# First x rows of a one-core decoder trunk: the norm columns in a transfer of their own, the first weight block in halves, two identity products ahead on TensorE

## The chip, the core and the metric

The kernel runs on one core of a Trainium2 chip. The metric is device time in microseconds (us) of one execution. Before the change three runs gave 1355.26 to 1356.71 us, with a median of 1356.11 us.

## What is computed

The reference is one layer of a hybrid decoder on 1024 tokens of width 1024, in f32. Cut to what the first stage of the kernel works on:

```python
def rmsnorm(x, w):
    y = x * lax.rsqrt(jnp.mean(x * x, axis=-1, keepdims=True) + EPS)
    return y * w

xn = rmsnorm(x, norm_mix_w[l])
proj = xn @ w_in[l]                 # 1024 x 4352
da_q, da_k, da_v, sw_q, sw_k, sw_v, g_da, g_sw = split_cols(proj)
...
merged = sigmoid(g_da) * (y_da @ w_br_da) + sigmoid(g_sw) * (y_sw @ w_br_sw)
x = x + merged @ w_mix_out
x = x + conv_ffn(rmsnorm(x, norm_ffn_w), w_up, conv_w, conv_b, w_down)
return rmsnorm(x, norm_final_w)
```

Behind the projection come differential attention with four heads, a sliding-window attention, the merge, and a gated MLP with a causal convolution. Only the start of the projection is changed.

## The kernel before, in words

**Layout.** The host lays x out transposed, in eight rows of tiles `xT[kc]` of 128 channels x 1024 tokens (512 KB each), and each weight matrix in blocks of 128 output columns (`w_in[m]`, 128 x 8 x 128, 512 KB). All small vectors lie in one array `vecs` of 128 partitions x 469 columns (234.5 KB). Its columns 0 to 7 are `norm_mix_w`, one column for each row of tiles; the other columns hold the other norms, the convolution, the sinks and the lambda vectors.

**Products in f32.** An f32 operand is split in two float32r parts, high and low. ScalarE writes the high part (a cast or a multiply), VectorE the low part (operand minus high part). A product is then three TensorE matmuls: high x high, low x high and high x low. In `load()` (L294) ScalarE writes `xh = x * w` (L301) and VectorE writes `xl` (L302), both with the column `wcol(kc)` of `vecs` (L317). In `load_w()` (L122) a weight block is transferred (L119) and split: `wh` on ScalarE (L129), `wl` on VectorE (L131). `split()` (L754) does the same for two given tiles. `blocks()` (L271) issues six matmuls for a weight block and an x row, three for each half of 512 tokens (L276 to L278).

**Order of the first stage, `project()` (L250).** The x rows are taken in the order 0, 4, 1, 5, 2, 6, 3, 7. The first is transferred in two halves of 512 tokens, with the whole first weight block between the two; the others are transferred whole. After row 4 the second weight block is loaded and multiplied with rows 0 and 4, after row 5 the third. Three weight blocks times eight rows times six are 144 matmuls, which accumulate in six PSUM banks. Beside them `square()` (L306) makes the sum of squares and multiplies x by the norm weights in place (L310 to L315), and `diffs()` and `parts()` (L280, L289) prepare differences and sums of x rows for the later pairs of weight blocks, which are multiplied with seven products instead of eight (`prods`). The sums over the partitions are taken by `col_sums` (L158: eight matmuls with f32 operands), then `rstd` is made and spread over the partitions (L173).

**PSUM.** The pool `psA` holds eight banks, taken in turn by one tag: six for the accumulations, then `ssq`, then the gate halves and the products of the pairs. When it closes, the attention's pools `psS`, `psG` and `psT` take the banks over, each new tile waiting for the last reader of the tile that was there.

**Queues and order.** x rows and weights are issued on SyncE's queue (SP), `vecs` on ScalarE's (L196). Waits and the order of instructions on each engine are put in by a framework that works from the dependences, with the place in the program as the priority: an instruction may be put ahead of others that stand before it in the program and whose inputs come later. `nsink` and `subw` (L442, L444), written at the beginning of the attention, read `vecs` on VectorE and stand first on that engine. `load_w` uses raw buffers of which there are three, and `xr` has six buffers, so later transfers wait for buffers.

The program's start (L184 to L196): the identity, `ones` and `mhalf` are made on GpSimd, `warm` makes ScalarE load its table, and `vecs` is transferred.

Of the kernel before, what the change touches and what calls it, by code (L numbers as in the profile page):

```python
# [10 lines left out]
F32 = mybir.dt.float32  # L11
F32R = mybir.dt.float32r
# [5 lines left out]
P = 128  # L18
D = 1024
T = 1024  # L20
KC = D // P
# [5 lines left out]
RAW = 3  # L27
# [15 lines left out]
class Trunk:  # L43
# [132 lines left out]
    def run(self):  # L176
        nc, tc = self.nc, self.tc
        with ExitStack() as ctx:

            for side, n in (("left", LPAD), ("right", RPAD)):  # L180
                pad = ctx.enter_context(tc.tile_pool(name=f"pad_{side}", bufs=1, side=side))
                pad.tile([P, n // 4], F32, name=f"pad_{side}_t")
            self.cp = ctx.enter_context(tc.tile_pool(name="cp", bufs=1))
            self.st = ctx.enter_context(tc.tile_pool(name="st", bufs=4))  # L184
            self.dp = ctx.enter_context(tc.tile_pool(name="dp", bufs=1, space=DRAM))
            self.ident = self.cp.tile([P, P], F32, name="ident")
            make_identity(nc, self.ident)
            self.ones = self.cp.tile([P, 1], F32, name="ones")
            nc.gpsimd.memset(self.ones, 1.0)
            self.mhalf = self.cp.tile([P, 8], F32, name="mhalf")  # L190
            nc.gpsimd.memset(self.mhalf, -0.5)
            self.vecs = self.cp.tile([P, NVEC], F32, name="vecs")

            warm = self.cp.tile([P, 1], F32, name="warm")
            nc.scalar.activation(warm, self.ones, AF.Exp)
            nc.scalar.dma_start(self.vecs, self.vecs_d)  # L196
            self.rstd = self.cp.tile([P, T], F32, name="rstd")
            self.gd = self.dp.tile([16, P, T], F32, name="gd")
            self.x2d = self.dp.tile([8, P, T], F32, name="x2d")
            self.hd = self.dp.tile([NF, P, T], F32, name="hd")  # L200
            self.yd = self.dp.tile([8, P, T], F32, name="yd")
            self.wp = ctx.enter_context(tc.tile_pool(name="wp", bufs=2))
            self.qd = self.dp.tile([18, 2, P, T], F32, name="qd")
            self.xctx = ExitStack()
            self.xp = self.xctx.enter_context(tc.tile_pool(name="xp", bufs=1, side="right", reuse_waits="tile"))
            self.plan()
            self.project()
            self.pctx = ExitStack()
            self.psS = self.pctx.enter_context(tc.tile_pool(name="psS", bufs=2, space=PSUM, reuse_waits="tile"))
            self.psG = self.pctx.enter_context(tc.tile_pool(name="psG", bufs=2, space=PSUM, reuse_waits="tile"))  # L210
            self.psT = self.pctx.enter_context(tc.tile_pool(name="psT", bufs=2, space=PSUM, reuse_waits="tile"))
            gctx = ExitStack()
            self.gpool = gctx.enter_context(tc.tile_pool(name="gp", bufs=2, reuse_waits="tile"))
            self.attention()
            self.rest(gctx)
# [34 lines left out]
    def project(self):  # L250
# [6 lines left out]
        with ExitStack() as ctx:  # L257
# [8 lines left out]
            rows = [k + 4 * i for k in range(4) for i in range(2)]  # L266
            xr, ws = {}, []
            bank = lambda: self.tl(psA, [P, H2], "t")
            ps = [[bank() for _ in range(2)] for _ in range(3)]

            def blocks(n, kcs):  # L271
# [21 lines left out]
            with tc.tile_pool(name="xrp", bufs=6, reuse_waits="tile") as xrp:  # L293
                def load(kc, cuts=((0, T),)):  # L294

                    x = xr[kc] = self.tl(xrp, [P, T], "xr")
                    for a, b in cuts:
                        nc.sync.dma_start(x[:, a:b], self.xT[kc, :, a:b])
                        if not ws:
                            ws.append(self.load_w(*self.wsrc.pop(0)))  # L300
                        nc.scalar.mul(self.xh[kc][:, a:b], x[:, a:b], wcol(kc))  # L301
                        nc.vector.scalar_tensor_tensor(self.xl[kc][:, a:b], x[:, a:b], wcol(kc), self.xh[kc][:, a:b].bitcast(F32), ALU.mult, ALU.subtract)  # L302
                    for n in range(len(ws)):
                        blocks(n, [kc])

                def square(kc):  # L306

                    x = xr[kc]
                    if kc == rows[0]:
                        nc.scalar.activation(acc, x, AF.Square)  # L310
                    else:
                        sq = self.tl(self.sfp[0], [P, T], "sf")
                        nc.scalar.activation(sq, x, AF.Square)
                        nc.vector.tensor_tensor(acc, acc, sq, ALU.add)
                    nc.scalar.mul(x, x, wcol(kc))  # L315

                wcol = lambda kc: self.vecs[:, C_NM + kc:C_NM + kc + 1]  # L317
                for i, kc in enumerate(rows[:6]):
                    load(kc, ((0, H2), (H2, T)) if i == 0 else ((0, T),))
                    if i in (1, 3):  # L320
                        ws.append(self.load_w(*self.wsrc.pop(0), pool=(self.uw, "sh", "sl") if i == 3 else None))
                        blocks(len(ws) - 1, rows[:i + 1])
                for kc in rows[:2]:
                    square(kc)
                diffs(0)
                for kc in rows[6:]:
                    load(kc)
                for kc in rows[2:]:
                    square(kc)
                ssq = bank()  # L330
                self.col_sums(ssq, [acc], NB, 0)
                rs = self.rstd_cols(ssq, 8, D)
                wg = self.next_w()
                pg = [bank()]
                for hf in range(2):
                    self.mm3(pg[0], wg, self.xact, 0, *((range(5), True, False), (range(5, KC), False, True))[hf])
                    self.spread(ssq, rs, hf * 4)
                    nc.vector.tensor_copy(self.rstd[:, hf * H2:(hf + 1) * H2], ssq)
                parts(0)
                for k in range(1, 4):  # L340
                    if k == 3:

                        us = [self.tl(xrp, [P, T], "xr") for _ in range(3)]
                        for hf in range(2):
                            for u, hv in zip(us, ps):
                                cols = slice(hf * H2, (hf + 1) * H2)
                                nc.vector.tensor_tensor(u[:, cols], hv[hf], self.rstd[:, cols], ALU.mult)
                    diffs(k)
                    parts(k)
                pg.append(bank())  # L350
                self.mm3(pg[1], wg, self.xact, 1)
                for m, u in zip(self.plain, us):
                    self.keep(m, u, (xrp, "xr"))
# [857 lines left out]
```

## Time and profile before

| | us |
|---|---|
| median of 3 runs (lowest, highest) | 1356.11 (1355.26, 1356.71) |
| the profiled execution, its own time | 1356.2 |
| its span, first to last instruction | 1354.3 |
| TensorE busy | 1335.0 (99%) |
| VectorE busy | 1009.8 (75%) |
| ScalarE busy | 603.9 (45%) |
| GpSimd busy | 483.1 (36%) |

The profile is of one execution. Times in it are microseconds from its first instruction; 1.9 us of the execution's own time lie outside the span. In a row of the timeline stand the start, the duration, the engine, the line of the kernel, the operation, output and inputs, and in brackets how long the engine had been idle and what released it. PE is TensorE, PEld its weight loads, DVE VectorE, ACT ScalarE, POOL GpSimd; ACTq and SPq are rows of transfers being issued. A view of stretches gives the busy time of each engine between two times, the granted TensorE clock, the share of time that the 16 DMA engines were busy, and GB/s. The chain of waits is followed back from the last instruction to what released each step.

### The profile page before, as it was taken

The page shows a single profiled execution, that of the slowest core. Times are in us where ns is not written, and L with a number is a line of the kernel's source. Part 1 is how long each engine was busy: PE and PEld are TensorE (multiplying, and loading weights), DVE is VectorE, ACT ScalarE, POOL GpSimd, SP SyncE. Part 2 cuts the span into 40 slices and gives each one's busy share as a digit, 9 for nine tenths or more (in the row PEclk, how much of TensorE's full clock was granted, in tenths as well). Part 3 has the DMA queues.
Part 4 walks back from the last instruction along what each step waited for, and adds up shares of the span by engine and source line. Part 5 has one row for each costly group of instructions (what it writes and reads, how often), then busy time and mean ns, then how long its engine had stood idle before and what let it go on. Part 6 is the DMA issues. An engine that isn't in the chain of part 4 may idle for free.

```text
span 1354.3 us, 17160 instructions
## 1 busy us (share of the span) xinstructions
PE 1335.0 (99%) x6304; PEld 1103.6 (81%) x6304; DVE 1009.8 (75%) x1454; ACT 603.9 (45%) x942; POOL 483.1 (36%) x350
## 2 busy tenths in 40 slices
PE   7999999999999999999999999999999999999997
PEld 6888888888887777878888888888888888888886
DVE  8846775388898875355689888888888898986454
ACT  8422232376667664334444334433443345433343
POOL 0436651010102125741455565555555611231011
PEclk9999999999999999999999999999999999999999
DMA  6334443966554235334422222122212248651342
GB/s 255 140 113 164 143 156 114 272 174 175 156 133 144 77 116 219 117 119 136 166 82 88 71 91 94 62 79 93 93 63 83 92 141 311 215 177 64 94 134 85
DMA packets 62470, 179.50 MB, mean 133 GB/s; under 512 B 6833, under 2 KB 15153, under 8 KB 62385
## 3 DMA queue, kind: packets, MB, share of 16 engines
q1 hardware_dynamic: 50928, 160.98, 36.7%
q10 hardware_dynamic: 11456, 17.41, 3.5%
q8 instruction: 50, 0.82, 0.2%
q14 instruction: 36, 0.29, 0.1%
HBM read 129.61 MB, written 48.76 MB: 132 GB/s over the span
## 4 chain that ended last, share of the span: by engine, by line
PE 62%; DVE 17%; POOL 7%; issue 7%; DMA 4%; ACT 3%; POOLq 0%; DVEq 0%; SPq 0%; ACTq 0%
PE t L836 7%; PE t L837 7%; PE t L835 7%; POOL us L965 3%; PE y L996 3%; PE d L996 3%; PE sc L568 3%; PE g L150 2%; PE g L151 2%; DVE c L958 2%; PE g L152 2%; DVE wl L112 2%; DMA gr<-gd 2%; PE sc L151 2%; PE sc L152 2%
## 5 line engine op out<-in xcount | busy, mean ns | idle before, releaser
L970 ACT ACTIVATE c<-us,vecs 128x1024 f32<-128x1024 f32 x44 | 54.8, 1248 | 163.2 <-POOL us L965 160.0
L965 POOL TENSOR_TENSOR us<-us,rstd 128x1024 f32<-128x1024 f32 x42 | 100.7, 2414 | 52.8 <-DVE wl L131 34.3
L110 ACT CAST sh<-sf 128x1024 fp32r<-128x1024 f32 x62 | 64.9, 1051 | 106.2 <-POOL sf L97 61.8
L129 ACT CAST wh<-raw 128x1024 fp32r<-128x1024 f32 (+2 forms) x60 | 60.7, 1012 | 104.8 <-PE sc L151 33.1
L971 DVE SCALAR_TENSOR_TENSOR c<-us,vecs,c 128x1024 f32<-128x1024 f32 x44 | 67.1, 1527 | 51.9 <-ACT c L970 51.9
L131 DVE TENSOR_TENSOR wl<-raw,wh 128x1024 fp32r<-128x1024 f32 (+2 forms) x60 | 75.3, 1256 | 39.1 <-ACT wh L129 29.3
L96 POOL TENSOR_TENSOR sf<-rv 128x512 f32<-128x512 f32 x30 | 42.5, 1417 | 166.7 <-DMA rv<-in_w_up 73.2
L112 DVE TENSOR_TENSOR sl<-sf,sh 128x1024 fp32r<-128x1024 f32 x62 | 88.3, 1426 | 8.2 <-ACT sh L110 8.2
L167 POOL TENSOR_TENSOR rs<-ms,mhalf 128x8 f32<-128x8 f32 (+2 forms) x9 | 14.5, 1614 | 159.1 <-DVE ms L165 148.5
L150 PE MATMUL g<-xh,wh 128*128 128x512 f32 x176 | 70.7, 402 | 0.1
L152 PE MATMUL g<-xh,wl 128*128 128x512 f32 x176 | 70.4, 400 | 0.0
L151 PE MATMUL g<-xl,wh 128*128 128x512 f32 x176 | 70.4, 400 | 0.0
L98 POOL TENSOR_TENSOR sf<-raw,rv 128x512 f32<-128x512 f32 x30 | 41.6, 1386 | 59.9 <-DVE sl L112 59.9
L572 DVE CUSTOM_DVE_ANT_0 L<-sc,bias 128x128 f32<-128x128 f32 (+7 forms) x64 | 47.7, 752 | 17.4 <-PE sc L568 14.1
L551 POOL MEMSET aT<- 128x128 f32 x32 | 6.1, 204 | 152.0 <-PE t L597 101.6
L573 ACT ACTIVATE L<-L,sm 128x128 f32<-128x128 f32 (+7 forms) x64 | 49.6, 778 | 20.7 <-DVE sm L572 18.2
L97 POOL TENSOR_TENSOR sf<-sf,raw 128x512 f32<-128x512 f32 x31 | 58.0, 1870 | 1.6
L972 DVE SCALAR_TENSOR_TENSOR c<-us,vecs,c 128x1024 f32<-128x1024 f32 x44 | 56.2, 1279 | 0.6
L725 POOL TENSOR_TENSOR gr<-gr,rstd 128x1024 f32<-128x1024 f32 x16 | 39.4, 2467 | 41.4 <-DMA gr<-gd 41.2
L112 DVE TENSOR_TENSOR wl<-raw,wh 128x1024 fp32r<-128x1024 f32 (+1 forms) x35 | 52.8, 1508 | 0.1
L151 PE MATMUL sc<-ml,wh 128*128 128x512 f32 x128 | 50.1, 391 | 0.6 <-DVE ml L746 0.6
L568 PE MATMUL sc<-u,u 128*128 128x512 f32 (+2 forms) x192 | 49.8, 359 | 0.1
(444 smaller groups left out, 4351.4 us busy)
## 6 DMA issues: line engine op xcount, KB each, us to landing
u<-qd SPq DMA_DIRECT2D x72, 256.0 KB, 6.1
raw<-in_w_down SPq DMA_DIRECT2D x27, 512.0 KB, 3.7
raw<-in_w_in SPq DMA_DIRECT2D x25, 512.0 KB, 4.4
hr<-hd SPq DMA_DIRECT2D x50, 256.0 KB, 5.3
raw<-in_w_up SPq DMA_DIRECT2D x23, 512.0 KB, 3.6
hd<-c SPq DMA_DIRECT2D x22, 512.0 KB, 2.8
rv<-in_w_up SPq DMA_DIRECT2D x21, 512.0 KB, 3.5
gr<-gd SPq DMA_DIRECT2D x16, 512.0 KB, 3.6
```

Of the source, the lines that this page charges most:

```text
L112: nc.vector.tensor_tensor(lo, src, hi.bitcast(F32), ALU.subtract)
L131: self.lo = (eng or nc.vector).tensor_tensor(wl, raw, wh.bitcast(F32), ALU.subtract)
L150: nc.tensor.matmul(ps, wh[:, kc + o, :], ah, start=first and n == 0, stop=False)
L151: nc.tensor.matmul(ps, wh[:, kc + o, :], al, start=False, stop=False)
L152: nc.tensor.matmul(ps, wl[:, kc + o, :], ah, start=False, stop=last and n == len(kcs) - 1)
L568: nc.tensor.matmul(sc[:, lo + n0:lo + n1], qs, k[c][part][:, n0:n1], start=part == 0, stop=part == 1)
L835: nc.tensor.matmul(ps, ah[:, k, :], bh, start=first and n == 0, stop=False, skip_group_check=skip)
L836: nc.tensor.matmul(ps, ah[:, k, :], bl, start=False, stop=False, skip_group_check=skip)
L837: nc.tensor.matmul(ps, al[:, k, :], bh, start=False, stop=last and n == len(ks) - 1, skip_group_check=skip)
L965: i = (nc.vector if m % NF == 0 else nc.gpsimd).tensor_tensor(us[:, 2:], us[:, 2:], self.rstd, ALU.mult)
L971: nc.vector.scalar_tensor_tensor(c, us[:, 1:T + 1], cw[1], c, ALU.mult, ALU.add)
L996: nc.tensor.matmul(ps, v[:, n, :], x, start=n == i == 0, stop=n == len(js) - 1 and i == 2)
```

## The change

Three edits, all ahead of the second x row. The transfer of `vecs` is cut in two: columns 0 to 7 alone, issued ahead of `warm`, and the other 461 columns, written in the program behind the split of the first weight block's second half, both on ScalarE's queue. The first weight block is transferred and split in two halves of four row tiles each: x half 0, weight half 0, x half 1, weight half 1, each 256 KB, and each weight half is split behind the x half that came before it. And a new PSUM tile `busy` is taken ahead of the six accumulators, and two matmuls write the product of the identity with itself, repeated four times (128 x 512, f32), into it; nothing reads it.

```diff
             self.vecs = self.cp.tile([P, NVEC], F32, name="vecs")
+            nc.scalar.dma_start(self.vecs[:, :KC], self.vecs_d[:, :KC])
             warm = self.cp.tile([P, 1], F32, name="warm")
             nc.scalar.activation(warm, self.ones, AF.Exp)
-            nc.scalar.dma_start(self.vecs, self.vecs_d)
...
             bank = lambda: self.tl(psA, [P, H2], "t")
+            busy = bank()
+            for _ in range(2):
+                nc.tensor.matmul(busy, self.ident, self.ident.unsqueeze(1).to_broadcast([P, 4, P]), start=True, stop=True)
             ps = [[bank() for _ in range(2)] for _ in range(3)]
...
                     for a, b in cuts:
                         nc.sync.dma_start(x[:, a:b], self.xT[kc, :, a:b])
-                        if not ws:
-                            ws.append(self.load_w(*self.wsrc.pop(0)))
+                        k0 = a // P if len(cuts) > 1 else None
+                        if k0 == 0:
+                            raw, wh, wl = (self.tl(self.wp, [P, KC, P], t, dt, **kw) for t, dt, kw in (("raw", F32, {"bufs": RAW}), ("wh", F32R, {}), ("wl", F32R, {})))
+                            ws.append((wh, wl))
+                            src = self.wsrc.pop(0)[0]
+                        if k0 is not None:
+                            nc.sync.dma_start(raw[:, k0:k0 + 4], src[:, k0:k0 + 4])
                         nc.scalar.mul(self.xh[kc][:, a:b], x[:, a:b], wcol(kc))
                         nc.vector.scalar_tensor_tensor(self.xl[kc][:, a:b], x[:, a:b], wcol(kc), self.xh[kc][:, a:b].bitcast(F32), ALU.mult, ALU.subtract)
+                        if k0 is not None:
+                            self.split(wh[:, k0:k0 + 4], wl[:, k0:k0 + 4], raw[:, k0:k0 + 4])
+                        if k0 == 4:
+                            nc.scalar.dma_start(self.vecs[:, KC:], self.vecs_d[:, KC:])
```

## The prediction

> **What bounds the kernel now.** I read the page first, then the table of stretches for the start, then the chain of waits, then TensorE's own rows.
>
> ```profile
> span 1354.3 us, 17160 instructions
> PE 1335.0 (99%) x6304; PEld 1103.6 (81%) x6304; DVE 1009.8 (75%) x1454; ACT 603.9 (45%) x942; POOL 483.1 (36%) x350
> ...
> 0.00:4.00 4.00, 0.00 (x0) 0.00 (x0) 0.00 (x0) 1.49 (x2) 0.77 (x8) 1.00 0.54 153
> 4.00:6.70 2.70, 0.00 (x0) 0.00 (x0) 0.98 (x3) 1.76 (x3) 0.00 (x0) 1.00 0.96 366
> 6.70:10.70 4.00, 3.85 (x9) 2.27 (x9) 3.24 (x4) 4.00 (x6) 0.00 (x0) 1.00 1.02 409
> 10.70:27.00 16.30, 16.30 (x72) 13.52 (x73) 16.20 (x17) 16.30 (x17) 0.00 (x0) 1.00 0.79 300
> ```
>
> TensorE is busy 99% of the span, and from 10.7 on without a gap. So what the start gains or loses is carried to the end, as long as nothing behind it eats it. The change touches only the first 10.7 us, where three other things are full: the DMA engines (0.96 and 1.02 of the time), and from 6.7 ScalarE, which stays full to 27.0. The chain of waits says which of them decides:
>
> ```profile
> 1.19 4.45 DMA raw<-in_w_in
> 5.66 1.04 ACT wh L129
> 6.71 0.62 ACT xh L301
> 7.33 0.95 ACT rstd L310
> 8.28 1.05 ACT xh L301
> 9.35 1.29 DVE xl L302
> 10.69 0.50 PE t L277
> ```
>
> It does not run over TensorE before 10.69. It runs over the weight block's landing at 5.64, ScalarE's queue up to the high part of row 4 (8.28), and VectorE's low part of row 4 (9.35). What TensorE does meanwhile stands in its rows and its waits:
>
> ```profile
> 6.76 0.80 PE L276 MATMUL t<-xh,wh 128*128 128x512 f32 x1 [6.76 <-ACT wh L129]
> ...
> 9.04 0.63 PE L277 MATMUL t<-xl,wh 128*128 128x512 f32 x1
> 9.47 0.63 PE L278 MATMUL t<-xh,wl 128*128 128x512 f32 x1
> 9.89 0.74 PE L276 MATMUL t<-xh,wh 128*128 128x512 f32 x2
> 10.69 0.50 PE L277 MATMUL t<-xl,wh 128*128 128x512 f32 x1
> ...
> 12.63 0.39 PE L276 MATMUL t<-xh,wh 128*128 128x512 f32 x1
> 12.86 0.39 PE L278 MATMUL t<-xh,wl 128*128 128x512 f32 x1
> ...
> PEld t L277 <- DVE xl L302: 0.6, 2, 0.5
> ```
>
> The first matmuls start 0.43 us apart (9.04, 9.47), the later ones 0.23 (12.63, 12.86): TensorE begins at about half pace, although the table gives the granted clock as 1.00 there. By 10.69 eight matmuls are done, and TensorE then waits some 0.5 us for row 4's `xl`. So the slow pace costs nothing now: the eight would have waited for the same `xl`. **The number that decides is when row 4's `xl` is ready, 10.69 now.**
>
> Row 4 is bound twice. Its transfer:
>
> ```profile
> xr<-in_xT SPq DMA_DIRECT2D x1, 256.0 KB, 3.6
> vecs<-in_vecs ACTq DMA_DIRECT2D x1, 234.5 KB, 3.8
> ...
> 1.66 0.90 SPq L298 DMA_DIRECT2D xr<-in_xT  x2
> ...
> xr<-in_xT SPq DMA_DIRECT2D x1, 512.0 KB, 6.0
> ```
>
> The pair at 1.66 is x half 1 and row 4, so row 4 is issued at about 2.1 and lands 6.0 later, at 8.1. And ScalarE:
>
> ```profile
> 0.73 0.41 ACTq L196 DMA_DIRECT2D vecs<-in_vecs  x1
> ...
> 2.47 0.20 ACT L195 ACTIVATE warm<-ones 128x1 f32<-128x1 f32 x1
> 4.56 0.72 ACT L301 ACTIVATE xh<-xr,vecs 128x512 fp32r<-128x512 f32 x1 [1.89 <-DMA vecs<-in_vecs]
> ...
> 6.61 0.72 ACT L301 ACTIVATE xh<-xr,vecs 128x512 fp32r<-128x512 f32 x1
> 7.24 1.04 ACT L310 ACTIVATE rstd<-xr 128x1024 f32<-128x1024 f32 x1
> 8.18 1.13 ACT L301 ACTIVATE xh<-xr,vecs 128x1024 fp32r<-128x1024 f32 x1
> ```
>
> It reaches row 4 at 8.18, 0.1 after the landing. Freeing ScalarE alone gains 0.1 us; the landing must come sooner too.
>
> **The change part by part.**
>
> *Eight columns first.* ScalarE waits at 4.56 for all of `vecs` (0.73 + 3.8); x half 0 has landed at 0.74 + 3.6 = 4.3. With 4 KB in place of 234.5 the bound is x half 0: at 4.3, or some 0.5 sooner if nothing shares the DMA engines with it (234.5 KB at the 409 GB/s of the table are 0.57 us). Gain at this place 0.2 to 0.8 us.
>
> *Halved weight block.* ScalarE's cast of 1024 columns is 1.04 us (L129) and a half is 1.04 - (1.13 - 0.72) = 0.63, so two halves add 0.22. On VectorE the rows are these:
>
> ```profile
> 4.56 0.17 DVE L442 TENSOR_SCALAR nsink<-vecs 128x8 f32<-128x8 f32 x1 [4.56 <-DMA vecs<-in_vecs]
> ...
> 9.35 1.28 DVE L302 SCALAR_TENSOR_TENSOR xl<-xr,vecs,xh 128x1024 fp32r<-128x1024 f32 x1 [0.72 <-ACT xh L301]
> 10.55 0.68 DVE L284 TENSOR_TENSOR xr<-xr 128x512 f32<-128x512 f32 x1
> 11.33 1.23 DVE L131 TENSOR_TENSOR wl<-raw,wh 128x1024 fp32r<-128x1024 f32 x1
> ```
>
> Two halves are 2 x 0.68 against 1.23, 0.13 more, hidden in the 0.72 idle ahead of 9.35; without that cover it would move `xl` by 0.13. SyncE issues one transfer more, at most 0.46 us (0.90 for two above), hidden because row 4 lies in the queue for 6 us. The first real matmul now waits for x half 0 and weight half 0: `xh` from 4.3 to 5.0, the half cast from there, first matmul at about 5.6 in place of 6.76, or 5.0 if x half 0 lands early. The six of row 0 are then done, even at 0.43, before 8.2. All this is earlier, and all of it waits for row 4.
>
> *Where row 4 lands.* Ahead of it lay 234.5 + 256 + 512 + 256 = 1258.5 KB. After the change the same bytes lie ahead, unless the rest of `vecs` (230.5 KB) is issued later. In the program it stands behind the second weight half. But the order on the engines is not that of the program: in before the `vecs` issue (L196) runs at 0.73 ahead of `warm` (L195, 2.47), which stands before it, and `nsink` (L442), written after the whole stage, is VectorE's first instruction. A transfer that waits for nothing is drawn forward in the same way. So I take it that the rest of `vecs` is issued right behind the eight columns, at about 1.2. Then row 4 lands at 8.1 as now; ScalarE, free at about 7.9 (4.3 plus 0.72, 0.63, 0.72, 0.63 and 1.04, each start some 0.1 ahead of the end before it), begins at 8.1 in place of 8.18. Sum: 0.1 us gained, at most 0.2.
>
> *Identity products.* No row shows a 512-column f32 product. The nearest is the f32 column sum:
>
> ```profile
> 41.65 1.84 PE L158 MATMUL t<-ones,rstd 128*128 128x1 f32 x16
> ```
>
> The code issues eight, the trace has sixteen records: an f32 product is two. Two identity products are then at least four records of 0.43 us, 1.7 us, from about 1.4 (the identity is made by GpSimd before 1.4) to 3.1; from above I allow them until 7.2, from where eight real matmuls at 0.43 would still be done at 10.6. As TensorE has nothing to do before 5.0 and waits for `xl` after it, their own cost is 0; their use is the pace from 10.6 on. The Trainium skill (FP8 and Floating Point Precision, TensorE Precision Notes) says that a true f32 product makes four passes; by it the two would take an estimated 3.4 us, until 4.8, and the sum would be the same.
>
> *The bank.* `busy` moves every later tile of `psA` by one bank, and the attention's tiles inherit other last readers, none later than `c21` (L402):
>
> ```profile
> 238.39 0.69 DVE L402 TENSOR_TENSOR us<-u,t 128x512 f32<-128x512 f32 x1 [0.51 <-PE t L837]
> ...
> 249.07 1.03 PE L538 MATMUL t<-ident,f 128*128 128x128 f32 x8
> ...
> 256.36 0.36 PE L568 MATMUL sc<-u,u 128*128 128x256 f32 x1
> ```
>
> `psT` starts at 249.07 and `psS` at 256.36, 10 us and more behind that reader, and `psG` inherits the tiles that are read earlier than now. Cost 0. The gate's second half inherits the same accumulator as before.
>
> **Sum.** 1356.2 for the profiled execution (span 1354.3 and 1.9 around it) less 0.1 is 1356.1; this execution is 0.1 above the median of the runs, so against the median I forecast **1356.0**. A measurement of this kernel tells about 0.2%, 2.7 us, from no change.
>
> **The rivals.**
>
> *The rest of vecs is issued late, as written (21%).* Then it lies behind row 4, which lands 0.57 us sooner, at 7.5. ScalarE has the second weight half at about 6.3, pays 0.41 for the issue and 0.95 for the square, and is free at 7.7. Gain 0.5 us: 1355.6. The stages behind let it pass: the second block's `wl` ends at 12.56 and is read at 12.86, and it moves up with VectorE's queue behind row 4. For it speaks the place in the program, against it L196 and L442.
>
> *The rest is late, and VectorE waits for it (13%).* `nsink` reads the rest and runs on an in-order engine. If the issue is at 6.3 and the landing takes 3.8 as now, it comes at 10.1. Should `nsink` stand ahead of row 4's `xl`, that one runs from 10.3 to 11.6 in place of 9.35 to 10.63: 1.0 us slower, 1357.2. Ahead of all the stage's low parts, it would hold five of them (0.75, 0.68, 0.75, 0.68, 1.28 less overlaps): `xl` at 14.2, 3.6 slower, 1359.8. It decides when `nsink` is put before `xl` and the landing is later than 9.3; 8 of the 13 are the mild form.
>
> *TensorE is still slow when row 4 comes (15%).* Now eight matmuls at 0.43 fall where they cost nothing, from 6.76 to at most 10.7, 3.9 us. After the change the identity products end long before row 4, and between lie only six to eight matmuls, about 3 us of work in some 5. If TensorE is then at half pace at 10.6, about eight matmuls of the dense row behind it take 0.20 longer each, 1.6 us, less the 0.1 gained: 1357.6, slower. It decides at the pace of the matmuls right behind row 4's `xl`. For it speaks the thin work from 5 to 10, against it that TensorE starts 5 us earlier than now. The Trainium skill (TensorE: Matmul & The Clock Gate, Part 1) gives the rule behind such a case: the clock is halved until about 3.4 us of sustained work have filled a free-running window, and falls back after an idle window; the before's 0.43 and 0.23 agree with it.
>
> *The order of a later stage changes (11%).* New first events can reorder ScalarE and VectorE up to 27, where both are full, by more than 2.7 us either way; slower 6, faster 5. Against it: TensorE finds its inputs in time throughout that stretch.
>
> **How the numbers follow.** The forecast has 40%, the rivals 21, 13, 15 and 11. The range leaves out the last rival and the strong form of the wait (16%), and reaches from the late issue's 1355.6, less 0.3 for its bounds and 0.7 for the spread of the runs, to the slow pace's 1357.6 with 0.6 of spread: 1354.6 to 1358.2. Faster by over 0.2%: 5% (the last rival). Slower: 6 and 5 from the strong wait, 11%. Within: 84%.
>
> **What would show it.** Right: the rest of `vecs` is issued before 2 us, row 4 lands at 8.0 to 8.2, its `xh` starts there, TensorE's first real matmul stands at 5.0 to 5.7, it waits about 1 us or more for row 4's `xl` at 10.5 to 10.7, and goes on at 0.23. Wrong: row 4's `xl` done before 10.3, matmuls 0.43 apart behind it, `nsink` idling VectorE ahead of it, or a PE gap after 27 that was not there.

## The result: slower, and most of the loss stands near 50 us, not at the start

The changed kernel took 1370.87 us, the median of five runs (1367.85 to 1371.55), beside 1356.11 (1355.26 to 1357.15) for the kernel before on the same chip: a ratio of 1.0099, 95% interval [1.0086, 1.0113]; by the medians it is 14.8 us slower. The profiled execution took 1368.09, 11.9 more than the profiled one of before (its span is 12.0 longer). Line numbers are shifted in the changed kernel: the matmuls L276 to L278 are L279 to L281, `xh` and `xl` L301 and L302 are L309 and L310, the copy of `rstd` L338 is L350, and row 0's multiply by the norm weights, L315, is L327.

The table of stretches of the changed kernel, with those of the prediction and two later ones (its span is 1366.3 us):

```profile
6.70:10.70 4.00, 1.28 (x4) 0.48 (x3) 2.13 (x3) 4.00 (x6) 0.00 (x0) 0.86 1.01 406
10.70:27.00 16.30, 15.68 (x58) 12.44 (x59) 16.22 (x16) 16.30 (x18) 0.00 (x0) 0.83 0.79 299
...
50.00:60.00 10.00, 4.73 (x22) 3.12 (x20) 4.25 (x4) 2.94 (x3) 8.63 (x7) 0.87 0.19 70
60.00:70.00 10.00, 8.94 (x33) 7.26 (x34) 7.74 (x11) 3.88 (x5) 4.01 (x3) 0.79 0.47 190
```

Two rows stand out. From 10.7 to 27.0 TensorE was busy without a gap before and made 72 matmuls; now it makes 58. And from 50 to 60 it is busy for 4.73 us of 10. VectorE and ScalarE are far from full there; only GpSimd is (8.63). The chain of waits of the changed kernel, first at the start (behind the landing of the second x half) and then at that hole:

```profile
6.48 0.72 ACT xh L309
7.20 0.83 ACT rstd L322
8.05 0.60 ACT wh L767
8.66 1.05 ACT xr L327
9.71 1.05 ACT xh L309
10.78 1.30 DVE xl L310
12.12 0.80 PE t L280
...
50.89 1.27 POOL sf L96
...
54.67 1.05 ACT sh L110
55.75 1.32 DVE sl L112
57.06 1.13 DVE t42l L768
58.20 0.60 DVE rstd L350
58.80 1.60 DVE sl L112
60.40 0.61 DVE rstd L350
```

At the start the chain runs over row 0's square (L322), the second half of the weight block (L767) and row 0's multiply (L327) before row 4's `xh`. In before, the multiply stood behind row 4. At the hole it runs over work for the first pair of weight blocks, which is needed much later: GpSimd's sums `sf`, ScalarE's `sh`, VectorE's `sl` (L112). Here one `sl` and a low part of an x difference (`t42l`) stand ahead of the first copy of `rstd` on VectorE, and another `sl` ahead of the second; each copy ends a wait of TensorE. The timelines of VectorE, before and then changed:

```profile
47.52 0.69 DVE L338 COPY rstd<-t 128x512 f32<-128x512 f32 x1 [0.76 <-PE t L173]
```

```profile
55.75 1.32 DVE L112 TENSOR_TENSOR sl<-sf,sh 128x1024 fp32r<-128x1024 f32 x1 [6.34 <-ACT sh L110]
...
58.12 0.68 DVE L350 COPY rstd<-t 128x512 f32<-128x512 f32 x1
```

Before, VectorE waited 0.76 us for TensorE's spread and copied at once. Now it stands still for 6.34 us in front of `sl`, while the copy's input has long been there (the first spread is at 50.97): it takes its instructions in order. TensorE's waits between 40 and 70 are then these two; in before its only wait there is one of 0.3:

```profile
PE t L173 <- DVE rstd L350: 5.2, 1, 5.2
PE t L150 <- DVE rstd L350: 1.1, 1, 1.1
```

TensorE's timelines, of the changed kernel and then two rows of before, give the sizes:

```profile
1.40 3.78 PE L271 MATMUL t<-ident 128*128 128x512 f32 x4 [1.40 <-POOL ident masks.py:199]
5.48 0.80 PE L279 MATMUL t<-xh,wh 128*128 128x512 f32 x1 [0.30 <-ACT wh L767]
...
10.80 0.80 PE L279 MATMUL t<-xh,wh 128*128 128x512 f32 x1 [2.03 <-ACT xh L309]
12.12 0.80 PE L280 MATMUL t<-xl,wh 128*128 128x512 f32 x1 [0.52 <-DVE xl L310]
...
45.32 1.84 PE L158 MATMUL t<-ones,rstd 128*128 128x1 f32 x16
...
50.97 0.65 PE L173 MATMUL t<-ident,rs 128*128 128x128 f32 x4
...
58.86 1.11 PE L173 MATMUL t<-ident,rs 128*128 128x128 f32 x4 [5.18 <-DVE rstd L350]
61.06 0.80 PE L150 MATMUL t<-xh,wh 128*128 128x512 f32 x1 [1.09 <-DVE rstd L350]
```

```profile
49.41 0.60 PE L173 MATMUL t<-ident,rs 128*128 128x128 f32 x4
...
50.35 0.50 PE L150 MATMUL t<-xh,wh 128*128 128x512 f32 x1 [0.34 <-DVE xr L347]
```

The column sums (L158) begin at 45.32 in place of 41.65: 3.7 us are lost by then. The matmul behind the second copy of `rstd` stands at 61.06; in before it stands at 50.35: 10.7 us are lost by then, 7.0 of them since the column sums, and 6.3 of these are the two waits. Seven matmuls behind 61.06 stand 0.43 apart in place of 0.23, another 1.4: 12.1. The ends of the two spans differ by 12.0, so what comes behind adds nothing on balance in this execution.

### The profile page after: what moved, and what is told of

Read it like the earlier page. It is cut to its first block, busy times and chain, and to the rows that moved or that the text cites. A ratio compares the mean times of both kernels' runs of the same rounds, so it can differ in the third digit from the quotient of the medians.

```text
span 1366.3 us, 17170 instructions
## 1 busy us (share of the span) xinstructions
PE 1343.0 (98%) x6308; PEld 1106.6 (81%) x6308; DVE 1011.6 (74%) x1455; ACT 603.9 (44%) x943; POOL 484.0 (35%) x350
## 4 chain that ended last, share of the span: by engine, by line
PE 69%; DVE 13%; POOL 7%; issue 5%; DMA 3%; ACT 2%; POOLq 0%; SPq 0%; DVEq 0%; ACTq 0%
PE t L849 9%; PE t L848 9%; PE t L847 9%; PE y L1008 3%; PE d L1008 3%; PE g L150 3%; PE sc L580 3%; PE g L151 3%; PE g L152 3%; POOL us L977 2%; DMA gr<-gd 2%; PE sc L151 2%; PE sc L152 2%; PE sc L150 2%; POOL gr L737 2%
## 5 line engine op out<-in xcount | busy, mean ns | idle before, releaser
L129 ACT CAST wh<-raw 128x1024 fp32r<-128x1024 f32 (+2 forms) x59 | 59.5, 1011 | 104.1 <-PE sc L151 33.1
L131 DVE TENSOR_TENSOR wl<-raw,wh 128x1024 fp32r<-128x1024 f32 (+2 forms) x59 | 75.7, 1282 | 37.6 <-ACT wh L129 27.9
L112 DVE TENSOR_TENSOR sl<-sf,sh 128x1024 fp32r<-128x1024 f32 x62 | 88.9, 1436 | 14.5 <-ACT sh L110 14.5
L112 DVE TENSOR_TENSOR wl<-raw,wh 128x1024 fp32r<-128x1024 f32 (+1 forms) x35 | 52.7, 1504 | 2.4 <-ACT wh L110 2.3
L737 POOL TENSOR_TENSOR gr<-gr,rstd 128x1024 f32<-128x1024 f32 x16 | 39.4, 2469 | 41.9 <-DMA gr<-gd 41.7
L152 PE MATMUL sc<-mh,wl 128*128 128x512 f32 x128 | 49.9, 390 | 0.0
```

Of the source, the lines that this page charges most:

```text
L112: nc.vector.tensor_tensor(lo, src, hi.bitcast(F32), ALU.subtract)
L131: self.lo = (eng or nc.vector).tensor_tensor(wl, raw, wh.bitcast(F32), ALU.subtract)
L152: nc.tensor.matmul(ps, wl[:, kc + o, :], ah, start=False, stop=last and n == len(kcs) - 1)
L737: i = nc.gpsimd.tensor_tensor(g, g, self.rstd, ALU.mult)
```

## The experiments

The theory after this reading was: two separate changes of order, one on ScalarE at the start and one on VectorE near 50, each with a slow pace of TensorE behind it. The rivals were that the late start itself makes the hole near 50, that the extra PSUM tile does, and that the identity products cost something of their own. Each kernel's loss below is its median less the median of before on its own chip.

**The three edits one by one.** First the vectors' transfer alone.

```diff
+            nc.scalar.dma_start(self.vecs[:, :KC], self.vecs_d[:, :KC])
             nc.scalar.activation(warm, self.ones, AF.Exp)
-            nc.scalar.dma_start(self.vecs, self.vecs_d)
...
+                            nc.scalar.dma_start(self.vecs[:, KC:], self.vecs_d[:, KC:])
```

> Only the split transfer of the vectors; the first weight block whole, no identity products. Theory of orders: on ScalarE and VectorE this edit leaves the order of before (row 4's high part ahead of the multiply of row 0 by its norm column, the copy of rstd ahead of the first pair's low parts), so the time stays within 1 us of before, row 4's low part is ready at 10.5 to 10.8 and TensorE waits nowhere over 0.5 us after it. Rival of the transfers: the small and the late transfer hold up row 4, its low part is ready after 11.3 and the time rises by 1 us or more.

It took 1356.89 us, ratio 1.0001 [0.9991, 1.001]: no difference. On ScalarE's timeline the first `xh` starts a microsecond sooner, and then ScalarE waits for the weight block that it waited for before, and row 4's `xh` starts at 8.17:

```profile
3.60 0.72 ACT L301 ACTIVATE xh<-xr,vecs 128x512 fp32r<-128x512 f32 x1 [0.93 <-DMA vecs<-in_vecs]
5.64 1.04 ACT L129 CAST wh<-raw 128x1024 fp32r<-128x1024 f32 x1 [1.32 <-DMA raw<-in_w_in]
...
8.17 1.13 ACT L301 ACTIVATE xh<-xr,vecs 128x1024 fp32r<-128x1024 f32 x1
```

Then the halves of the weight block alone (the same lines of the change, without the two transfers of `vecs` and without `busy`).

> Only the halved first weight block; the vectors in one transfer, no identity products. Theory of orders: the halves put the second half's cast and the multiply of row 0 (1.14 us) ahead of row 4's high part on ScalarE, and a difference (0.68 us) ahead of its low part on VectorE, so row 4's low part is ready at about 12 in place of 10.7, and the time rises by 1 to 2.5 us; the copy of rstd still stands ahead of the first pair's low parts, so TensorE waits at most 1 us for it near 50. Rival, all of the loss is in the transfers of the halves: 8 us or more of the 14.8 show here. Rival, the loss is the identity products' alone: no change within 0.5 us.

It took 1361.21, ratio 1.0031 [1.0019, 1.0043]: 4.5 us slower, more than the 1 to 2.5 expected. Row 0's multiply stands ahead of row 4 on ScalarE, as in the changed kernel, and the column sums begin at 44.36. And here too VectorE's order near 50 is another, a milder one:

```profile
47.87 1.22 DVE L763 TENSOR_TENSOR t13l<-xr,t13h 128x1024 fp32r<-128x1024 f32 x1
49.01 2.30 DVE L763 TENSOR_TENSOR t42l<-xr,t42h 128x1024 fp32r<-128x1024 f32 x1
...
52.92 0.68 DVE L345 COPY rstd<-t 128x512 f32<-128x512 f32 x1
```

Low parts and differences of x rows, all needed later, stand ahead of the copy, and TensorE waits 1.4 us for it and 1.0 us for the step behind it, where at most 1 was expected. Then the identity products alone (`busy` and the two matmuls).

> Only the two identity products. Theory of orders: they leave the start's order, row 4's low part is ready at 10.7 as before, but on VectorE a low part of the first pair of weight blocks now stands ahead of the first copy of rstd, so TensorE waits 3 to 6 us for that copy near 55, loses its pace once more (matmuls 0.43 us apart for some 3 us), and the time rises by 5 to 9 us. Rival, the identity products cost only through TensorE's pace in the first 16 us: the time rises by 1 to 3 us and no wait near 55 grows. Rival, the loss lies in the halves: no change within 0.5 us.

It took 1368.12, ratio 1.0086 [1.0069, 1.0103]: 11.4 us slower, over the 5 to 9 expected, although nothing reads what they write. The column sums begin at 42.10, only 0.45 late. The loss lies behind them, in TensorE's waits between 40 and 70:

```profile
PE t L150 <- DVE xr L350: 1.8, 1, 1.8
PE t L173 <- DVE rstd L341: 1.4, 1, 1.4
PE t L152 <- DVE wl L131: 0.9, 1, 0.9
PE t L150 <- ACT wh L129: 0.6, 1, 0.6
```

These sum to 4.7, and TensorE goes at 0.43 from 44.6 to 51.4 and again behind 58.5. VectorE has the changed kernel's order: it stands still for 5.73 us in front of an `sl` that is ahead of the first copy of `rstd`. So the hole does not need the late start: here the column sums are hardly late. The last two rows, first in time, are a second change of order. They concern the gate block, the weight block that is multiplied behind the column sums: its high and low part (L129, L131) stand behind casts and low parts of x rows that stood behind them before. The three losses sum to 0.2 + 4.5 + 11.4 = 16.1, near the 14.8 of all together. So one edit, the products, makes most of the loss when it is tried alone.

**Bank or products.** The extra PSUM tile without the products:

```diff
+            busy = bank()
             ps = [[bank() for _ in range(2)] for _ in range(3)]
```

> The kernel before with the extra PSUM tile taken ahead of the six accumulators, and no product of the identity. All later tiles of that pool move by one bank, and the order of instructions on VectorE and ScalarE is that of before. Theory (the products change the order of the work near 50 us, the bank costs nothing): 1355.5 to 1357.3, ratio within 0.1% of before, and no wait of TensorE near 50 over 1 us. Rival (the loss comes with the moved banks, whose new tiles wait for other last readers): 1360 or more, with waits behind 50 us that before does not have.

It took 1356.31, ratio 1.0005 [0.9996, 1.0014]: the moved banks cost nothing measurable, and TensorE's one wait between 40 and 70 is that of before (0.3). The rival of the banks is out.

**The order near 50 in the changed kernel.** Only the place of `sl`, and of the last low part of x differences, is forced back behind the second copy of `rstd`; what is computed stays.

```diff
-                    nc.vector.tensor_copy(self.rstd[:, hf * H2:(hf + 1) * H2], ssq)
+                    spread_out = nc.vector.tensor_copy(self.rstd[:, hf * H2:(hf + 1) * H2], ssq)
...
-                    parts(k)
+                    with tc.issue_after(spread_out.ins) if k == 3 else nullcontext():
+                        parts(k)
...
-                    with tc.issue_after(self.pow.ins):
+                    with tc.issue_after(self.pow.ins), tc.issue_after(spread_out.ins):
                         wg, pg = self.next_w(), [bank() for _ in range(2)]
```

> The changed kernel with one thing more: the first pair's low parts, and the last low part of the x differences, must stand behind the second copy of rstd on VectorE. Theory of orders: the waits of 5.2 and 1.1 us for that copy go, and with them the second slow stretch of TensorE (1.4 us); of the 14.8 us 7 to 10 come back, and what stays, 3.5 to 7 us, lies ahead of 46 in the span. Rival, the waits for the copy are only where an earlier delay comes out (the start's): less than 3 us come back.

It took 1360.19, ratio 1.0025 [1.0015, 1.0034]: the loss falls from 14.8 to 3.5 us, and TensorE has no wait left between 40 and 70. In VectorE's timeline the copy again waits for TensorE and not TensorE for it:

```profile
50.22 0.69 DVE L350 COPY rstd<-t 128x512 f32<-128x512 f32 x1 [2.18 <-PE t L173]
```

So 11.3 of the 14.8 us hang on that order on VectorE, the slow pace behind its waits included.

**The order at the start.** Row 0's multiply is forced behind row 4's `xh` on ScalarE, in the changed kernel and in the one just told:

```diff
-                        nc.scalar.mul(self.xh[kc][:, a:b], x[:, a:b], wcol(kc))
+                        xr[kc, 0] = nc.scalar.mul(self.xh[kc][:, a:b], x[:, a:b], wcol(kc))
...
-                    nc.scalar.mul(x, x, wcol(kc))
+                    with tc.issue_after(xr[rows[1], 0].ins) if kc == rows[0] else nullcontext():
+                        nc.scalar.mul(x, x, wcol(kc))
```

> The changed kernel with one order forced: row 0's multiply by the norm column stands behind the high part of row 4 on ScalarE, as it did before; all that is computed stays. Theory (two separate orders, one at the start and one near 50 us): ScalarE begins row 4's high part at its landing, about 8.5, in place of 9.61, the low part is done near 11.0 and TensorE's second matmul of row 4 stands at 11.0 to 11.2 in place of 12.12; the column sums begin 0.9 to 1.3 us earlier, and the low part of the first pair still stands ahead of the copies of rstd, so the time is 1369 to 1370, 0.2% over 1 us below the changed kernel and still 12 to 13.5 us above the kernel before. Rival (the loss near 50 comes from the late start itself): with the start mended the waits near 50 shrink too, and more than 4 us come back, 1366 or less. Rival (the start is absorbed by slack behind it): 1370.9 unchanged although row 4 comes earlier.

It took 1367.89, ratio 1.0083 [1.0069, 1.0096]. The hole near 50 stays (waits of 3.7 and 1.6 us). This run says little on whether a late start makes it, since the column sums still begin at 45.03 in place of 45.32; the kernel with the products alone, 0.45 late and with the same order, says more. The gain of some 3 us over the changed kernel is larger than expected, but the two intervals overlap.

> The changed kernel with both orders forced: row 0's multiply behind row 4's high part on ScalarE, and the first pair's low parts behind the second copy of rstd on VectorE. Theory: no wait near 50, and row 4's low part at about 11.0 in place of 12.1; against 1360.2 with the second order alone 0.9 to 1.3 us come back, 1358.9 to 1359.3, and what is left over the kernel before, some 2 to 2.8 us, is row 4's landing at 8.5 in place of 8.1 (0.3 to 0.4) and the slow pace of eight matmuls behind row 4 (about 1.4). Rival (the order on ScalarE is the whole of the start's loss): 1356 to 1357. Rival (the start's order costs nothing): 1360.2.

It took 1359.9, ratio 1.0024 [1.0013, 1.0034], the same as without the new order at the start (3.5 us of loss in both). Row 4's `xh` does start at its landing, at 8.60, and its `xl` product stands at 11.12 in place of 11.46. But the matmuls behind it stand 0.43 apart until 16.83, where they had done so until 14.83. The earlier row 4 was paid back by the pace, and the third outcome, that this order costs nothing measurable, is the one that holds.

**The pace.** Three more identity products are put behind row 0's products, in the gap in which TensorE waits for row 4; they write the tile that nothing reads (`xr["last"]` is the last of row 0's products):

```diff
+                    if i == 0:
+                        with tc.issue_after(xr["last"].ins):
+                            for _ in range(3):
+                                nc.tensor.matmul(busy, self.ident, self.ident.unsqueeze(1).to_broadcast([P, 4, P]), start=True, stop=True)
```

> As the kernel with the low parts behind the second copy of rstd, and three more products of the identity (six records) put right behind row 0's products on TensorE, so that TensorE works from 8.1 to about 11 instead of standing idle for 2.03 and 0.82 us; row 0's multiply stays ahead of row 4's high part. Theory (the pace falls because TensorE has little to do ahead of row 4): the matmuls behind row 4's low part at 11.5 are 0.23 apart from the first on in place of 0.43, and 1.3 to 1.6 us come back: 1358.6 to 1359.0 in place of 1360.2. Rival (the pace is no matter of idle time): still 0.43 behind row 4, 1360.2. Rival (the products run at half pace, 0.95 us a record): they end near 14 and hold row 4 up, 1362 to 1363.

The pace came as the theory says. TensorE's timelines behind row 4, first without the three products and then with them:

```profile
11.46 0.59 PE L280 MATMUL t<-xl,wh 128*128 128x512 f32 x1 [0.82 <-DVE xl L310]
...
12.27 0.63 PE L279 MATMUL t<-xh,wh 128*128 128x512 f32 x1
12.70 0.63 PE L280 MATMUL t<-xl,wh 128*128 128x512 f32 x1
```

```profile
7.73 2.74 PE L335 MATMUL t<-ident 128*128 128x512 f32 x6
...
11.71 0.50 PE L280 MATMUL t<-xl,wh 128*128 128x512 f32 x1 [0.82 <-DVE xl L310]
12.05 0.40 PE L281 MATMUL t<-xh,wl 128*128 128x512 f32 x1
12.28 0.40 PE L279 MATMUL t<-xh,wh 128*128 128x512 f32 x1
```

The rows behind stand 0.43 apart in the one until 14.83, and 0.23 from 12.05 on in the other, and the column sums begin at 42.93 in place of 44.22, the 1.3 us of the theory. But the time is 1363.48, ratio 1.0048 [1.0035, 1.0061], 3.6 us of loss more than without the products. None of the three outcomes foresaw this; the third comes near it in time, but the products ended at 10.5 and not near 14. TensorE came sooner to the gate block and met the second change of order, as in the kernel with the products alone:

```profile
PE t L150 <- ACT wh L129: 1.5, 1, 1.5
PE t L152 <- DVE wl L131: 0.5, 1, 0.5
```

So that order was there in the changed kernel as well, hidden by the late start. It is forced back here, with the three products kept:

```diff
+                wg_high, wg_low = self.hi, self.lo
...
-                    diffs(k)
+                    with tc.issue_after(wg_low.ins) if k == 3 else nullcontext():
+                        diffs(k)
+                    with tc.issue_after(wg_high.ins) if k >= 2 else nullcontext(), tc.issue_after(wg_low.ins) if k >= 2 else nullcontext(), ...
                         parts(k)
```

> As the kernel with three more products of the identity behind row 0's (1363.5), with the gate block's high and low part also put ahead of the last casts, low parts and differences of x rows. Theory (there the start was mended, and TensorE then came to the gate block before its casts: waits of 1.45 and 0.53 near 46 us and a slow pace behind them): the column sums stand at about 42.9 again, those waits go, TensorE keeps the pace of 0.23 through 45 to 60, and 4 to 6 us come back: 1357.3 to 1359.0, which is the 1.3 us by which the column sums are later than before (41.65), and at most 1 more. Rival (the loss of that kernel lies behind 60, in the waits for a transfer of 1.1 us and others): 1361 or more, with no wait near 46.

It took 1359.33, ratio 1.0029 [1.0018, 1.004]: 3.5 us came back where 4 to 6 were expected, the waits near 46 are gone and the pace is 0.23 from row 4 on. The median lies 0.3 above the expected range. In the profiled execution the second half of x row 0 landed late (its `xh` at 7.26, against 5.59 in the kernel above), row 4's `xl` product stands at 12.90, and the column sums at 44.1.

**The products with before's order.** The same three constraints in the kernel with the products alone:

> The kernel before with the identity products alone, and the order near 50 us forced to be nearly that of before: the gate block's high and low part stand ahead of the last two groups of casts and low parts of x differences, the last differences behind the gate block's low part, and the first pair's low parts behind the second copy of rstd. All that is computed stays. Theory (the products' whole cost lies in these orders): of the 11.4 us that the products alone cost, at least 10 come back, 1355.5 to 1358; TensorE has no wait over 0.6 us between 42 and 62. Rival (a part of the loss is the products' own, by bank or clock): 1360 or more, with TensorE at full pace from row 4 on and no wait near 50. Rival (the forced orders hold up other work): 1359 or more, with waits between 55 and 80 that before does not have.

It took 1358.18, ratio 1.0019 [1.001, 1.0029]: the loss falls from 11.4 to 2.4, so 9.0 came back where at least 10 were expected. TensorE's only wait between 40 and 70 is one of 0.6 (before: 0.3). The column sums begin at 42.4, 0.8 late, and the profiled execution has another wait of 1.6 for a transfer at the attention's beginning. The orders are four fifths of the products' cost; what the rest is, these runs do not settle.

**The halves with before's order**, the constraint on row 0's multiply included:

> The kernel before with the first weight block in halves alone (4.5 us slower when it was tried), and with all orders forced to be nearly those of before: row 0's multiply behind row 4's high part on ScalarE, the gate block's parts ahead of the last casts, low parts and differences, the first pair's low parts behind the second copy of rstd. Theory (the halves' cost is orders for the most part, too, and the rest is row 4's later landing and the slow pace behind it): no wait near 50 over 0.7 us, column sums at 42.5 to 44, 1357.0 to 1358.8. Rival (all of it is orders): 1355.3 to 1356.8. Rival (none of it): 1360 or more.

It took 1358.57, ratio 1.0014 [1.0005, 1.0023]: the loss falls from 4.5 to 2.4, inside the first theory's range. The column sums begin at 44.6, beyond the expected 42.5 to 44, in a profiled execution that is the slowest of the eleven (1359.83). ScalarE's timeline shows what is left in it:

```profile
7.49 0.72 ACT L306 ACTIVATE xh<-xr,vecs 128x512 fp32r<-128x512 f32 x1 [1.81 <-DMA xr<-in_xT]
...
9.89 1.15 ACT L306 ACTIVATE xh<-xr,vecs 128x1024 fp32r<-128x1024 f32 x1 [0.22 <-DMA xr<-in_xT]
```

The second x half comes at 7.49 and row 4 at 9.89 (before: 6.61 without a wait, and 8.18).

**Late columns.** The other 461 columns are issued behind row 4's `xh`, in the kernel with both orders, and then once more with the fillers and the gate block's order:

```diff
+                    if i == 1:
+                        with tc.issue_after(xr[kc, 0].ins):
+                            nc.scalar.dma_start(self.vecs[:, KC:], self.vecs_d[:, KC:])
```

> Both orders forced as in the kernel with two orders, and the other 461 columns of the vectors issued on ScalarE behind row 4's high part, as the program's text has it late. Theory: the 230.5 KB no longer lie ahead of row 4, which lands 0.5 to 0.6 us sooner (about 7.9 in place of 8.5); ScalarE is then the bound (free at about 8.0), row 4's low part is done at about 10.5 and 0.4 to 0.6 us come back against the kernel with two orders: 1358.3 to 1358.8. Rival (VectorE waits for the late columns): the columns land near 13, and if the sinks' scaling stands ahead of low parts of the second block or row 1, TensorE waits 1 to 3 us near 13: 1360 to 1362. Rival (the landing does not bind): same as the kernel with two orders.

It took 1360.98, ratio 1.004 [1.0027, 1.0054]. Row 4's `xh` starts at 8.00 in place of 8.60 and its `xl` product stands at 10.52, as expected; but the time did not fall. The matmuls behind row 4 stand 0.43 apart until 15.8, and the column sums begin at 44.30. VectorE stands still for 1.79 us for the late columns (`nsink` at 13.99), but at that pace TensorE does not wait for it; the time lies in that rival's range without its wait.

> The changed kernel with everything mended that the runs pointed to: three more identity products behind row 0's, the rest of the vectors issued behind row 4's high part, row 0's multiply behind it, the gate block's parts early, the first pair's low parts behind the second copy of rstd. Theory: row 4's high part starts at about 8.0, TensorE's second matmul of row 4 stands at 10.5 to 11 and keeps 0.23 from there, the column sums stand at 41.7 to 42.2 and the time is 1356.2 to 1357.5: no better than before, because before also has its dense matmuls from 10.7 on. Rival (a better start is worth its length): column sums before 41.4 and 1355.5 or less, faster than before. Rival (the fillers hold row 4 up, as they end at about 10.4): column sums at 42.5 or later, 1357.5 to 1358.5.

It took 1359.36, ratio 1.0029 [1.002, 1.0039], not the expected 1356.2 to 1357.5; no version beat the kernel before. The column sums begin at 44.16 in place of the expected 41.7 to 42.2, for two reasons. Row 4's `xh` waited for its landing until 9.08 and not 8.0, so that TensorE's second matmul of row 4 stands at 11.61. And VectorE's timeline has the wait of the prediction's second rival, ahead of row 1 and not of row 4:

```profile
15.58 0.17 DVE L463 TENSOR_SCALAR nsink<-vecs 128x8 f32<-128x8 f32 x1 [2.29 <-DMA vecs<-in_vecs]
...
15.73 2.47 DVE L310 SCALAR_TENSOR_TENSOR xl<-xr,vecs,xh 128x1024 fp32r<-128x1024 f32 x2
```

The late columns hold VectorE for 2.29 us ahead of row 1's `xl`, and TensorE then waits 1.07 us for it.

**Two groups of times.** The changed kernel's five runs lie near 1368 and near 1371. It was profiled twice more.

> The changed kernel itself, looked at once more, since its times fall near 1368 and near 1371. Theory (the length of the slow stretch behind row 4 and the landings of the first 2 MB decide which): the column sums begin at 45 to 46 when the time is near 1368, and 1.5 to 3 us later, with a longer run of matmuls 0.43 apart, when it is near 1371; the waits near 50 to 62 sum to 6 to 8 us in both. Rival (the slow stretches near 60 differ): column sums at the same place within 0.5, and the matmuls 0.43 apart last longer behind 61. Rival (a later stage differs): the same places up to 70, and the difference lies behind.

> The changed kernel a third time, with the same expectations as for the second look: near 1371 the column sums at 46.5 to 48.5 by the theory of the start, or the stretch behind 61 longer by the first rival, or a difference behind 70 by the second; near 1368 no difference over 0.5 us at any of the three places.

These took 1371.87 and 1370.16. Two stretches of TensorE alone, the second profile from 0 to 20 and then the third from 60 to 70 (busy time, matmuls, granted clock, share of the DMA engines, GB/s):

```profile
0.00:20.00 20.00, 16.09 (x35) 1.00 0.82 304
```

```profile
60.00:70.00 10.00, 8.91 (x29) 0.65 0.45 182
```

The column sums begin at 45.8 and 45.2 (first profile: 45.3), so the theory of the start falls. In the third profile 1.1 of the 2.0 us by which its span is longer come from the slow stretch behind 61: its matmuls stand 0.43 apart until 66.6 and not until 64.2, and the granted clock from 60 to 70 is 0.65 in place of 0.79. In the second profile only 0.5 of the 3.8 us by which its span is longer lie ahead of 418; 2.3 lie between there and 713, the rest behind. So there is no single place, and the groups stay open.

## Why the prediction was wrong

**The step that failed** is the one that carries the start to the end: "what the start gains or loses is carried to the end, as long as nothing behind it eats it". The forecast put a change of order behind 27 us at nothing. The nearest rival, "the order of a later stage changes" (11%), names the mechanism but stops at 27, and my reason against it was: "TensorE finds its inputs in time throughout that stretch". That is true of before, and is a statement on before's order only. In its place the runs show the order on VectorE between 50 and 61: 11.3 of the 14.8 us come back when it alone is forced back. Of my signs of being wrong, "a PE gap after 27 that was not there" is the one that came, with gaps of 5.18 and 1.09 us.

Before's profile had the slack. VectorE's first copy runs from 47.52 to 48.21, and the second spread, which waits for it in the changed kernel, stands at 49.41. So some 1.2 us fit between them, and an `sl` that starts at 55.75 does not. I costed the edits by what they do to times and not by what they do to the order: I cited L196 and L442 as proof that the framework moves instructions, used it for the transfer and for `nsink`, and took before's order for the rest.

**ScalarE's queue at the start** was costed as "free at about 7.9", a sum of five instructions without row 0's multiply. (With the overlaps that it names the sum gives about 7.6; the landing at 8.1 bound either way.) The chain of the changed kernel has the multiply (1.05) in it, and the second x half's `xh` starts at 6.48, so row 4's `xh` started at 9.61 and not 8.1. By itself this order cost nothing measurable (1359.9 with it mended, 1360.19 without).

**The landing.** I took row 4 at 8.1, since the bytes ahead of it are the same. With the multiply moved away, its `xh` waited for the transfer until 8.60 in one profile and 8.99 in another, and 9.89 with the halves alone. The second x half's start lay anywhere from 5.59 to 7.49 in these kernels. This term of the sum was too small by 0.5 to 1.8 us.

**The pace.** "TensorE is still slow when row 4 comes" (15%, priced at 1.6 us) was right as a mechanism. The distance from row 4's `xl` product to the column sums tells it in one number:

| kernel | `xl` product of row 4 | column sums | distance |
|---|---|---|---|
| before | 10.69 | 41.65 | 31.0 |
| changed | 12.12 | 45.32 | 33.2 |
| VectorE's copy first | 11.46 | 44.22 | 32.8 |
| both orders | 11.12 | 45.1 | 34.0 |
| copy first, three more products | 11.71 | 42.93 | 31.2 |

In before, one matmul more of row 4 was done by then, so 0.2 of each distance below the first row is no matter of pace. The rest of the growth is 1.6 to 2.8 us in the three kernels without products ahead of row 4, as much as I priced or more, and the identity products at 1.4 do not prevent it; three such products right ahead of row 4 do. The Trainium skill (TensorE: Matmul & The Clock Gate, Part 1) says that the clock falls back after an idle window of about 3.4 us; here waits of 2.03 and 0.52 us with one matmul between them were enough, so by this trace the gap need not be one of 3.4 us.

**What was right.** The vectors' rest was drawn forward (issued at 1.24), the first x row's gains all went into the wait for row 4, the first real matmul stood at 5.48 (forecast 5.0 to 5.7), and the moved banks cost nothing measurable. The identity products took 3.78 us, over my lower bound of 1.7 and done before the first real matmul. The Trainium skill's four passes (FP8 and Floating Point Precision, TensorE Precision Notes; an estimate of 3.4) agree better with this trace. That the change gains next to nothing when no order moves is not shown: every version with orders forced back keeps a loss, and with everything mended that the runs pointed to the time was still 1359.36.

**What stays open.** The 2.4 to 4.6 us that the mended kernels keep are not split into terms. In those with the halves in them most of it is at the start: in their profiles the column sums begin at 44.1 to 45.1, 2.4 to 3.4 us late. With the products alone they begin 0.8 late. Later landing, slow pace and waits take part, and removing one of them let another through. And why a product that nothing reads makes the framework order two engines differently 40 us later is not shown by any run; that it does, and that the bank alone does not, is.

## What to carry to other kernels

Where a framework orders the instructions, an edit at the start can be paid for far behind it: compare each in-order engine's order of instructions of the two kernels before costing anything, and look at once for an instruction with a late input that has moved ahead of one that TensorE waits for. Then pin the few orders that count by explicit constraints, and only then judge the edit. That TensorE is never late in a stage shows that the order it has works, and nothing of another order: ask for each instruction that TensorE waits for how late it may come (1.2 us here).

## What the runs showed of the hardware

TensorE's pace fell to half (0.43 us in place of 0.23 for 512 columns) behind some short waits (2.03 and 0.82 ahead of row 4, 5.18 and 1.09 near 60, and in the kernel with the products alone 0.64 behind the column sums), and stayed there for 3.1 to 5.7 us of dense matmuls (61.06 to 64.20, 11.46 to 14.83, 61.30 to 66.59, 11.12 to 16.83). It did not fall behind each: after waits of 1.38 and 1.02 near 55 in the kernel with the halves alone, and after one of 1.07 at 17.05 in the last mended kernel, the matmuls stand 0.23 apart. So no length of a wait that decides comes out of these runs. The granted clock of the table does not always tell: it reads 1.00 from 0 to 20 in the second profile of the changed kernel, whose matmuls stand 0.43 apart until 17.3, and 0.83 in the first, where they do so until 16.1. An f32 product of 128 x 512 took 0.91 us at full pace (2.74 for three) and 1.89 at half pace (3.78 for two). The products that filled the gap ahead of row 4 kept the pace, while those at the start ran at half pace for all of their 3.78 us.
